# 32 unused columns behind the channel vectors of a two-layer hybrid encoder kernel: all tiles behind x lie 128 bytes further on

## The chip, the core and the metric

The kernel runs on one core of a Trainium2 chip. TensorE (PE in the profile) does the matrix products and loads their stationary operand with separate instructions (PEld). VectorE (DVE), ScalarE (ACT) and GpSimd (POOL) do the rest; SyncE (SP) issues most DMAs. On-chip memory (SBUF) has 128 partitions, and a tile takes the same stretch of addresses in each of them. The metric is the time of one execution on the device, in microseconds, lower is better.

## The reference

Two layers over 256 tokens of width 1024, then a last RMSNorm; all in float32:

```python
def hybrid_layer(x, ...):
    h = rms_norm(x, g_mix)
    proj = h @ w_in                                   # 1024 x 8704
    b_a, c_a, x_a, u_p, q, k, v, ga, gp, gt = jnp.split(proj, split_points(), axis=-1)
    y_a = short_conv_mixer(b_a, c_a, x_a, conv_w, w_a_out)
    y_p = multiscale_pool_mixer(u_p, w_pool, pool_scale)
    y_t = windowed_gqa(q, k, v, rel_bias, sink) @ w_attn_out
    merged = sigmoid(ga) * y_a + sigmoid(gp) * y_p + sigmoid(gt) * y_t
    x = x + merged @ w_o
    h2 = rms_norm(x, g_ffn)
    gate, up = jnp.split(h2 @ w_gu, [D_FF], axis=-1)
    return x + (silu(gate) * up) @ w_down
```

The convolution has three taps, the pool mixer averages over windows of 2 to 16 tokens, and the attention has 16 heads of 64 over 4 key heads.

## The kernel before, in words

**Layout.** The activations stand transposed: 128 channels on the partitions, 256 tokens along the row. The kernel cuts each weight matrix into blocks of 128 x 128; the host packs all blocks in the order of their use (`plan_layer`) into the array `wst`, 16 blocks (1 MB) to a chunk.

**Three products for one.** A float32 product is made of three matmuls in the rounded type float32r: a value is split into a rounded part (hi) and the rest (lo), and `mm3` (L163 to L167) adds W_hi·X_hi, W_hi·X_lo and W_lo·X_hi in PSUM. So each block of weights costs three matmuls of 256 columns, on L165, L166 and L167. Each matmul is preceded by a load of its weights. ScalarE and VectorE split the weights (`convert`, L131: raw to hi on ScalarE, raw minus hi to lo on VectorE) and the activations (`split`, L237).

**Order.** `take` walks over the plan; at each half chunk `advance` issues the DMAs of chunks to come (up to three raw buffers) and the conversion of half chunks to come (five hi and five lo buffers). The order of all other work is that of the program.

**Stages of a layer.** In the mixer: key and value projections, queries, gates, the convolution branch (c, y, z), the attention interleaved with it (`att_scores`, tile sc, L355 and L356, with weights in q and moving kk; `att_transpose`, tile pt, L384; `att_pv`, tile o, L399, with weights in vt and moving ph and pl), the pool branch (up, pp), and the merge (m, wo). Then the feed-forward part: gate and up from xg and h, down from fa (dn). The last layer's down projection has fa as its weights and moves hi and lo, 512 columns at a time (L625 to L627). While no normalised activations are there yet, the matmuls use xg, x times the norm's gain, and the norm's factor comes in later; afterwards they use h.

**Places in SBUF.** The pools are laid out in the order `const`, `wp`, `act`, `tmp`, each tile behind the one before. In bytes per partition: `wp` holds 3 raw tiles of 8192, 5 hi and 5 lo of 4096. `act` begins with the tile x (`xc`, L185): 2144 floats, that is 8576 bytes, the first 96 (`NG`) of them the channel vectors `ch` (gains, convolution taps and pool scales of both layers), the others the activations x, 8 x 256. Behind x come 8 tiles kk of 1024, 2 tiles up of 1088, 2 tiles vt of 2048, and then the pairs of 2048 bytes (a hi half and a lo half of 1024 each): xg, z and m (tag xz), q, ao and fa (tag q), ga and ya, h, pp. `tmp` follows with 8 tiles of 2048 (tag t2: s, ph, pl, sq, sg, fs and others), 10 of 1024 (tag t1), the bias tiles and small ones.

**Loads at the start.** `dma_chunk` for the first two chunks (L119 to L126) alternates pieces of x with pieces of the weights on SyncE's queue: first the channel vectors with the first 256 columns of x (L123), then four blocks of weights, and so on. In DRAM the array `xT` has one row per partition, laid out as the tile is.

Of the kernel before, what the change touches and what calls it, by code (L numbers as in the profile page):

```python
# [16 lines left out]
P = 128  # L17
D = 1024
T = 256
L = 2  # L20
KT = D // P
# [14 lines left out]
def plan_layer(last):  # L36

    out = []

    def inner(mat, ns, nk=KT):  # L40
        for n in ns:
            for k in range(nk):
                out.append((mat, k, n))

    def outer(mat, ns, nk=KT):
        for k in range(nk):
            for n in ns:
                out.append((mat, k, n))

    outer("in", (CK, CK + 1, CV, CV + 1))  # L50
    for q in range(2):
        inner("in", [CQ + 4 * q + j for j in range(4)])
    inner("in", [CGA + n for n in range(8)])
    for n in range(8):
        inner("in", (CC + n, CX + n, CB + n))
    inner("in", (CU, CU + 1))
    inner("a", range(8))
    for n in range(8):
        inner("in", (CGP + n, CGT + n))
        if n % 2 == 1 and n < 7:  # L60
            inner("in", (CU + n + 1, CU + n + 2))
        inner("t", (n,))
        out.extend(("pool", k, n) for k in range(2))
        if n >= 2:
            out.extend(("o", n - 2, m) for m in range(8))
    for j in range(4):
        out.extend(("o", k, m) for k in (6, 7) for m in (2 * j, 2 * j + 1))
    for q in range(NQ):
        ns = (2 * q, 2 * q + 1, FT + 2 * q, FT + 2 * q + 1)
        if q == 0:  # L70
            outer("gu", ns)
        else:
            inner("gu", ns)
        if q >= 1:
            for k in (2 * q - 2, 2 * q - 1):
                out.extend(("down", k, m) for m in range(8))
    ks = (2 * NQ - 2, 2 * NQ - 1)
    if last:
        for k in ks:
            out.extend(("down", k, m) for m in range(8))  # L80
    else:
        for j in range(4):
            out.extend(("down", k, m) for k in ks for m in (2 * j, 2 * j + 1))
    return out


NCH = len(plan_layer(False)) * L // CT
NG = L * 6 * KT


@with_exitstack
def trunk(ctx, tc, wst, xT, sinkb, rb, invc, gfin, ident_d, out):
# [24 lines left out]
    def dma_chunk(c):  # L117
        raw = wp.tile([P, CT * P], F32, name=f"raw{c}", tag="raw", bufs=3)
        if c < 2:  # L119
            for a, b, xa, xb in (((0, 4, 0, 1), (4, 8, 1, 2), (8, 16, 2, 4)), ((0, 8, 4, 6), (8, 16, 6, 8)))[c]:  # L120
                s = slice(0 if xa == 0 else NG + xa * T, NG + xb * T)
                if xa == 0:
                    nc.sync.dma_start(xc[:, s], xT[:, s])  # L123
                nc.sync.dma_start(raw[:, a * P:b * P], wst[c, :, a * P:b * P])
                if xa > 0:
                    nc.sync.dma_start(xc[:, s], xT[:, s])  # L126
        else:
            nc.sync.dma_start(raw, wst[c])
        raws[c] = raw
# [53 lines left out]
        PE.matmul(wps[:, :T], warm[:, :P], warm, start=True, stop=True)  # L183

    xc = act.tile([P, NG + KT * T], F32, name="x")  # L185
    ch = xc[:, :NG].rearrange("p (l g k) -> p l g k", l=L, g=6)
    x = xc[:, NG:].rearrange("p (k t) -> p k t", k=KT)
    dma_chunk(0)
    dma_chunk(1)
# [657 lines left out]
```

## Time and profile before

| | |
|---|---|
| runs shown | 986.62, 987.08 and 987.37 us, median 987.08 |
| the profiled execution | 987.34 us |
| its span, from first to last instruction | 985.2 us |
| granted TensorE clock, mean | 0.998 of full |
| HBM read | 175.80 MB, 180 GB/s over the span |
| hi and lo conversions of weights | 322 of each |
| DMA queue of SyncE: share of the 16 engines | 48.4% |

How to read the lines of the profile that follow. A group reads: line, engine, operation, what it writes <- what it reads (buffer numbers left out), shape written <- shape read, xcount | busy us, mean ns of one | idle time of the engine just before them, and what ended it. For a matmul the mean is from its start to its modelled end, so that it overlaps with the next; the pitch, from one start to the next, is shorter. In the windows view a row holds the stretch, its length, then busy time and count for PE, PEld, DVE, ACT and, where it has work, POOL, the granted clock, the DMA engines' share and GB/s; its last row holds the sums over the stretches. In the view of a single line or tile, three numbers with slashes are the shortest, the median and the longest duration in ns. In the timeline a row has start (us), duration (us), engine, line, operation, tiles and how many were merged. In the chain a row has start, duration and what it was.

### The profile page before, as it was taken

To read this page: it belongs to the slowest core of one execution; us is meant where nothing else is said; L and a number is where in the kernel's file an instruction comes from. 1 tells how busy PE (TensorE), PEld (TensorE's weight loads), DVE (VectorE), ACT (ScalarE), POOL (GpSimd) and SP (SyncE) were. 2 spreads that over 40 slices of the span, in tenths; PEclk is the share of its full clock that TensorE was granted. 3 is DMA by queue.
4 is the path that set the end of the run, shared out by engine and by line. 5 is a ranking of instruction groups with operands and counts; after the bars stand their busy time and mean duration, and the time that the engine had idled before them with its cause. 6 is when DMAs were issued, how large, how long until landed. Compare 5 with 4: busy or idle time off the path is not lost.

```text
span 985.2 us, 19117 instructions
## 1 busy us (share of the span) xinstructions
PE 975.4 (99%) x7881; PEld 963.1 (98%) x7881; DVE 712.6 (72%) x1277; ACT 553.5 (56%) x916; POOL 37.1 (4%) x60
## 2 busy tenths in 40 slices
PE   8999999999999999999999999999999999999997
PEld 8999999999999999999999999999999999999996
DVE  7899898577668955545589888975667697555555
ACT  6766666655456544444577566765544574444443
POOL 4000000000001000000020000000000020000000
PEclk9999999999999999999999999999999999999999
DMA  8656545544554555455543745444555455645531
GB/s 302 237 187 211 180 160 165 199 173 172 195 190 172 172 185 199 172 175 194 187 172 129 241 157 178 148 172 166 180 192 189 173 186 179 214 172 177 195 142 43
DMA packets 26967, 178.11 MB, mean 181 GB/s; under 512 B 3136, under 2 KB 3664, under 8 KB 6656
## 3 DMA queue, kind: packets, MB, share of 16 engines
q1 hardware_dynamic: 24768, 169.93, 48.4%
q0 software_dynamic: 2112, 6.97, 2.6%
q8 instruction: 61, 1.00, 0.4%
q14 instruction: 26, 0.21, 0.1%
HBM read 175.80 MB, written 1.08 MB: 180 GB/s over the span
## 4 chain that ended last, share of the span: by engine, by line
PE 98%; DMA 1%; DVE 0%; ACT 0%; SPq 0%; issue 0%
PE b L166 25%; PE b L165 25%; PE b L167 25%; PE dn L167 2%; PE dn L166 2%; PE dn L165 2%; PE dn L626 2%; PE dn L625 2%; PE dn L627 2%; PE wo L165 2%; PE wo L166 2%; PE o L399 2%; PE wo L167 2%; PE pt L384 1%; PE sc L356 1%; PE sc L355 1%
## 5 line engine op out<-in xcount | busy, mean ns | idle before, releaser
L139 DVE TENSOR_TENSOR lo<-raw,hi 128x1024 fp32r<-128x1024 f32 (+1 forms) x322 | 390.5, 1221 | 215.1 <-ACT hi L138 214.9
L138 ACT ACTIVATE hi<-raw 128x1024 fp32r<-128x1024 f32 (+1 forms) x322 | 337.1, 1053 | 337.5 <-PE b L166 213.1
L165 PE MATMUL b<-h,hi 128*128 128x256 f32 x1344 | 381.5, 284 | 0.0
L166 PE MATMUL b<-h,hi 128*128 128x256 f32 x1344 | 380.2, 283 | 0.0
L167 PE MATMUL b<-h,lo 128*128 128x256 f32 x1344 | 380.2, 283 | 0.0
L166 PEld LDWEIGHTS b<-h,hi 128*128 128x128 f32 x1344 | 257.9, 192 | 0.2
L165 PEld LDWEIGHTS b<-h,hi 128*128 128x128 f32 x1344 | 257.8, 192 | 0.2
L167 PEld LDWEIGHTS b<-h,lo 128*128 128x128 f32 x1344 | 257.8, 192 | 0.0
L166 PE MATMUL b<-xg,hi 128*128 128x256 f32 x448 | 127.0, 284 | 0.8 <-DVE xg L255 0.8
L165 PE MATMUL b<-xg,hi 128*128 128x256 f32 x448 | 127.2, 284 | 0.3 <-DVE xg L252 0.3
L167 PE MATMUL b<-xg,lo 128*128 128x256 f32 x448 | 126.8, 283 | 0.2 <-DVE lo L139 0.2
L166 PEld LDWEIGHTS b<-xg,hi 128*128 128x128 f32 x448 | 85.9, 192 | 1.4 <-DVE xg L255 1.3
L165 PEld LDWEIGHTS b<-xg,hi 128*128 128x128 f32 x448 | 85.8, 192 | 0.6 <-issue 0.5
L167 PEld LDWEIGHTS b<-xg,lo 128*128 128x128 f32 x448 | 85.9, 192 | 0.4 <-DVE lo L139 0.4
L165 PE MATMUL dn<-fa,hi 128*128 128x256 f32 x176 | 49.8, 283 | 0.0
L166 PE MATMUL dn<-fa,hi 128*128 128x256 f32 x176 | 49.8, 283 | 0.0
L167 PE MATMUL dn<-fa,lo 128*128 128x256 f32 x176 | 49.8, 283 | 0.0
L368 ACT ACTIVATE s<-s,sm 128x256 f32<-128x256 f32 x64 | 31.8, 499 | 13.0 <-DVE sm L363 13.0
L165 PE MATMUL b<-z,hi 128*128 128x256 f32 x128 | 36.5, 285 | 0.0
L165 PE MATMUL b<-ao,hi 128*128 128x256 f32 x128 | 36.2, 283 | 0.0
L166 PE MATMUL b<-ao,hi 128*128 128x256 f32 x128 | 36.2, 283 | 0.0
L167 PE MATMUL b<-ao,lo 128*128 128x256 f32 x128 | 36.2, 283 | 0.0
(176 smaller groups left out, 1500.5 us busy)
## 6 DMA issues: line engine op xcount, KB each, us to landing
raw<-wst SPq DMA_DIRECT2D x158, 1024.0 KB, 4.9
bias<-stab POOLq DMA_DIRECT2D x16, 384.0 KB, 4.2
raw<-wst SPq DMA_DIRECT2D x3, 512.0 KB, 8.0
out<-yg SPq DMA_DIRECT2D x4, 256.0 KB, 2.2
x<-xT SPq DMA_DIRECT2D x3, 256.0 KB, 8.0
raw<-wst SPq DMA_DIRECT2D x2, 256.0 KB, 4.6
gf<-gfin POOLq DMA_DIRECT2D x2, 256.0 KB, 2.9
x<-xT SPq DMA_DIRECT2D x1, 176.0 KB, 2.3
```

The lines of the kernel that those rows point to most:

```text
L138: S.activation(hi[:, s], raw[:, s], AF.Copy)
L139: V.tensor_tensor(lo[:, s], raw[:, s], hi[:, s].bitcast(F32), op=ALU.subtract)
L165: PE.matmul(dst, wh, xh, start=start, stop=False, skip_group_check=skip)
L166: PE.matmul(dst, wh, xl, start=False, stop=False, skip_group_check=skip)
L167: last_mm[0] = PE.matmul(dst, wl, xh, start=False, stop=stop, skip_group_check=skip)
L355: PE.matmul(ps[:, half(j)], qs[t][j][:, cs], kh, start=True, stop=False)
L356: PE.matmul(ps[:, half(j)], qs[t][j][:, cs], kl, start=False, stop=True)
L368: S.activation(ss[i // 2][:, i % 2], ss[i // 2][:, i % 2], AF.Exp, bias=sm[:, 4 + i:5 + i], accum_out=sm[:, 12 + i:13 + i])
L399: PE.matmul(ps[:, half(j)], vv, pts[kt][i][:, half(j)], start=(kt == i == 0), stop=(kt == i == 1))
L625: PE.matmul(d, ah[:, cs], wh, start=(k == 0), stop=False)
L626: PE.matmul(d, ah[:, cs], wl, start=False, stop=False)
L627: PE.matmul(d, al[:, cs], wh, start=False, stop=(k == FT - 1))
```

## The change

`NG` grows from 96 to 128 floats: the tile x gets 32 columns between the channel vectors and the activations that nothing reads. The channel vectors keep their place, the activations x and each tile allocated behind it move by 128 bytes per partition; const, raw, hi and lo stay. The host puts zeros into the same columns of `xT`, whose rows grow from 8576 to 8704 bytes. The first load of x takes the new columns along (384 floats per partition in place of 352). No instruction is added, removed or reordered.

```diff
-NG = L * 6 * KT
+
+NG = L * 6 * KT + 32
...
     xc = act.tile([P, NG + KT * T], F32, name="x")
-    ch = xc[:, :NG].rearrange("p (l g k) -> p l g k", l=L, g=6)
+    ch = xc[:, :L * 6 * KT].rearrange("p (l g k) -> p l g k", l=L, g=6)
     x = xc[:, NG:].rearrange("p (k t) -> p k t", k=KT)
...
-    xT = np.ascontiguousarray(np.concatenate([chp.reshape(P, NG), xT.reshape(P, KT * T)], axis=1))
+    xT = np.ascontiguousarray(np.concatenate([chp.reshape(P, L * 6 * KT), np.zeros((P, NG - L * 6 * KT), chp.dtype), xT.reshape(P, KT * T)], axis=1))
```

## The prediction

> **What bounds the kernel now.** I read the page first: span, busy times, granted clock, and the chain that ended last.
>
> ```profile
> span 985.2 us, 19117 instructions
> ...
> PE 975.4 (99%) x7881; PEld 963.1 (98%) x7881; DVE 712.6 (72%) x1277; ACT 553.5 (56%) x916; POOL 37.1 (4%) x60
> ...
> PEclk9999999999999999999999999999999999999999
> ...
> PE 98%; DMA 1%; DVE 0%; ACT 0%; SPq 0%; issue 0%
> ```
>
> TensorE is busy 99% of the time at the full granted clock, and the chain that sets the end runs over it for 98%. So only what TensorE itself needs per matmul can matter much; VectorE (72%) and ScalarE (56%) have room. How many matmuls of the main kind there are stands in the groups by line and shape:
>
> ```profile
> L165 PE MATMUL b<-h,hi 128*128 128x256 f32 x1344 | 381.5, 284 | 0.0
> ...
> L165 PE MATMUL b<-xg,hi 128*128 128x256 f32 x448 | 127.2, 284 | 0.3 <-DVE xg L252 0.3
> ...
> L165 PE MATMUL dn<-fa,hi 128*128 128x256 f32 x176 | 49.8, 283 | 0.0
> L165 PE MATMUL b<-z,hi 128*128 128x256 f32 x128 | 36.5, 285 | 0.0
> L165 PE MATMUL b<-ao,hi 128*128 128x256 f32 x128 | 36.2, 283 | 0.0
> ...
> L165 PE MATMUL wo<-m,hi 128*128 128x256 f32 x128 | 35.4, 284 | 0.0
> ...
> L165 PE MATMUL b<-pp,hi 128*128 128x256 f32 x32 | 9.1, 283 | 0.0
> ```
>
> These are 2384 on L165, and as many each on L166 and L167: 7152 matmuls of 256 columns. All have their weights in hi or lo and their moving operand in a tile behind x. One nanosecond more or less per matmul is 7.15 us, 0.72% of the time. This is the sensitivity on which everything below hangs.
>
> **The change, part by part.** It adds and removes no instruction, wait or queue entry. It makes the first x load larger, and it changes addresses. Take as a tile's *place* its distance behind the first weight tile, modulo 512 bytes, worked out from the tile sizes in the order of the pools. A weight block is 512 bytes wide, so every block of hi and lo is at place 0. Before, x begins at 0 and is 8 x 1024 + 384 bytes long, so the eight kk tiles are at 384; the two up tiles are 1088 bytes each, so vt and everything after (xg, z, m, q, ao, fa, h, pp, s, ph, pl) are at 384 + 2 x 64 = 512, that is 0 again. After, kk is at 0 and all those at 128. So today the weights and the moving operand of all 7152 matmuls begin at the same place, and after the change the moving operand begins 128 bytes off.
>
> Does TensorE see that? The trace holds a comparison of its own. The attention's P·V matmuls (L399, tile o) have weights in vt and move ph or pl: same place. The score matmuls (L355 and L356, tile sc) have weights in q and move kk: 384 against 0, that is 128 bytes off in the other direction. Both come in runs of 8, have 256 columns, use each weight block twice in a row, and are preceded by ordinary matmuls. The weight loads, by line and shape:
>
> ```profile
> L166 PEld LDWEIGHTS b<-h,hi 128*128 128x128 f32 x1344 | 257.9, 192 | 0.2
> ...
> L399 PEld LDWEIGHTS o<-ph,vt 128*128 128x128 f32 x64 | 12.3, 192 | 0.0
> ...
> L355 PEld LDWEIGHTS sc<-kk,q 128*128 128x128 f32 x64 | 12.1, 189 | 0.0
> ```
>
> 192 ns at the same place, 189 ns off it. For the pitch I take the busy time of TensorE on the tile kk alone and on vt alone, in windows that hold whole runs (first the stretch, then busy time and count):
>
> ```profile
> sum 210.00, PE 15.62 PEld 14.29 DVE 0.00 ACT 0.00; mean PE 7.81 PEld 7.15 DVE 0.00 ACT 0.00
> ```
>
> ```profile
> sum 260.00, PE 17.97 PEld 16.51 DVE 0.00 ACT 0.00; mean PE 8.98 PEld 8.26 DVE 0.00 ACT 0.00
> ```
>
> A run's busy time is seven pitches and the last matmul's own duration, whose median stands in the view of each line:
>
> ```profile
> L355 PE MATMUL sc<-kk,q x64: 279/282/285, 58.8 to 649.8; 128*128 128x256 f32 x64
> ```
>
> ```profile
> L399 PE MATMUL o<-ph,vt x64: 283/283/283, 78.9 to 669.9; 128*128 128x256 f32 x64
> ```
>
> The kk windows hold 14 runs: (15.62/14 - 0.282)/7 = 119.1 ns. The vt windows hold 16: (17.97/16 - 0.283)/7 = 120.0 ns. Moreover, o never varies (283/283/283), and sc does (279 to 285). I read this so: at the same place the loads of weights and the stream of the moving operand, which run at the same time, settle into one fixed rhythm of 120 ns that is a little slower than the free one; off it they don't. The same free rhythm shows for a moment after an interruption, in the timeline of TensorE (start, duration):
>
> ```profile
> 26.28 0.63 PE L303 MATMUL ps<-ident,rr 128*128 128x256 f32 x4
> 26.75 0.28 PE L165 MATMUL b<-xg,hi 128*128 128x256 f32 x1
> ...
> 27.70 0.28 PE L167 MATMUL b<-xg,lo 128*128 128x256 f32 x1
> ```
>
> From 26.28 to 27.70 there are 12 matmuls: 118.3 ns each. Afterwards they are back at 0.12.
>
> *Main matmuls.* Nearest row: sc, the one steady pattern with the operands 128 bytes apart. 7152 x (120.0 - 119.1) = 6.4 us less. Bounds: nothing, if the rhythm stays; 7152 x (120.0 - 118.3) = 12.2 us less, if the free rhythm lasts; and above, if each matmul took as long as sc's slowest (285 against 283), 7152 x 2 = 14.3 us more. I take 6.4.
>
> The Trainium skill speaks against this term: "TensorE: Matmul & The Clock Gate", section "Step-by-step: what each phase is for", says that TensorE reads its two operands from SBUF over independent ports and that loading the next weights takes nothing from the running matmul. By that this term is 0 and the time stays at 987.1. The trace does not quite agree: 119.1 against 120.0 ns between sc and o.
>
> *Other matmuls.* o: vt, ph and pl move together, no change. sc: q to 128, kk to 0, still 128 apart, no change. The last layer's down projection has its weights in fa, which moves, and its moving operand in hi, which doesn't:
>
> ```profile
> L625 PE MATMUL dn<-hi,fa 128*128 128x512 f32 x88 | 34.4, 390 | 0.0
> ...
> L625 PEld LDWEIGHTS dn<-hi,fa 128*128 128x128 f32 x88 | 16.6, 188 | 3.2
> ```
>
> Its weight loads are already at the short 188 ns, so I count 0; with 2 ns either way for its 264 it is 0.5 us.
>
> *VectorE, ScalarE, GpSimd.* Their operands move too. The hi and lo split of kk (place 384) and of h (place 0) tells whether they care:
>
> ```profile
> L239 DVE TENSOR_TENSOR h<-hf,h 128x256 fp32r<-128x256 f32 x32 | 12.3, 422 | 0.0
> ...
> L238 ACT ACTIVATE h<-hf 128x256 fp32r<-128x256 f32 x32 | 12.2, 413 | 5.3 <-DVE hf L314 5.1
> ...
> L239 DVE TENSOR_TENSOR kk<-kf,kk 64x256 fp32r<-64x256 f32 x8 | 3.4, 419 | 2.2 <-ACT kk L238 1.9
> L427 ACT ACTIVATE kk<-kf 64x256 fp32r<-64x256 f32 x8 | 3.3, 417 | 0.2
> ```
>
> 419 against 422 and 417 against 413 ns: no effect that shows. What could come late next is the weights' conversion, which shares these engines; at 72% and 56% busy it follows a matmul stream that is under 2% quicker. Without that cover the gain would stop there.
>
> *The loads at the start.* The first x load grows from 352 to 384 floats per partition, 176 to 192 KB, ahead of the weight loads in SyncE's queue; the chain and the issues:
>
> ```profile
> 2.59 6.40 DMA raw<-wst
> 9.02 0.64 ACT hi L138
> ```
>
> ```profile
> x<-xT SPq DMA_DIRECT2D x1, 176.0 KB, 2.3
> ```
>
> ```profile
> 0.00:30.00 30.00, 27.44 (x205) 26.43 (x206) 22.26 (x46) 19.22 (x29) 11.49 (x33) 1.00 0.91 322
> ```
>
> The chain waits for a raw load until 9.0 us, and the DMA engines move 322 GB/s meanwhile: 16.4 KB more is 0.05 us. Upper bound: in proportion to that load's 2.3 us, 0.2 us. Below, x's rows begin elsewhere in DRAM and SBUF; no row prices it, and I allow 0.2 us of gain. I take 0.05.
>
> *Sum.* The profiled execution took 987.34 us, 985.2 of it the span. 987.34 - 6.4 + 0.05 = 981.0. The median of the runs is 0.26 lower, hence 980.8, 0.6% faster.
>
> **The rivals.**
> *Longer free rhythm.* If the main stream runs free as it does after an interruption, 12.2 us: 975. For it: sc's runs are only 8 long and start out of the fixed rhythm. Against: that stretch falls back to 0.12 by itself.
> *Nothing changes.* The rhythm of 120 ns holds at any place, and sc differs for another reason, say that half of kk's partitions hold copies or zeros, or that runs of 8 are too short to settle. Or the change isn't what it says, since tiles are laid out otherwise than I worked out. Then 987.1. For it: almost all of the weight loads are at 192 ns, and after each interruption they return there. Against: o, from the same start, never leaves it, and sc leaves it each time.
> *Slower.* The main matmuls lock at another rhythm: the loads of weights collide with the moving stream for longer at +128 bytes, as sc has -128 and modulo 512 these differ. Place: L165 to L167. Price: up to 2 ns, sc's slowest duration, 14.3 us, so 1001; at half of that 994. It decides from a pitch over 120.3 ns, where 7152 x 0.3 is 0.2%. For it: sc reaches 285 ns. Against: its mean is lower.
>
> **How the numbers follow.** Forecast, 119.1 ns: 0.34. Free rhythm: 0.23. Nothing: 0.26. Slower: 0.17. The range goes from 973 (the free rhythm less 2 us for the starts and the last layer's matmuls) to 988.5 (nothing, and the bounds of the small terms), which leaves out the slower case and little else. About 0.2%, 2 us, is what a measurement of this kernel can tell from no change. Faster 0.57, same 0.26, slower 0.17.
>
> **What would show it.** If I am right, the weight loads of L165 to L167 fall from 192 to 187 to 190 ns, their matmuls' durations begin to vary, sc keeps 189 and 119.1, and the gain spreads evenly over the span, while the start (first 30 us) and the end stay. If the loads stay at 192 the time is unchanged. If they grow, the slower case has come. The forecast is wrong if the gain comes from the start, or if VectorE's or ScalarE's groups change their mean.

## The result, and the profile after

| | before | after |
|---|---|---|
| median on the device | 986.93 us (986.62 to 987.37, 4 runs) | 979.87 us (979.42 to 980.07, 4 runs) |
| span of the profiled execution | 985.2 us | 977.7 us |

The ratio is 0.9927, with a 95% interval of 0.991 to 0.9945: 0.7% faster. The forecast was 980.8 us.

The page of the changed kernel, in the lines that answer to those shown of before:

```profile
span 977.7 us, 19117 instructions
...
PE 968.2 (99%) x7881; PEld 954.9 (98%) x7881; DVE 712.1 (73%) x1277; ACT 552.7 (57%) x916; POOL 38.0 (4%) x60
...
PEclk9999999999999999999999999999999999999999
...
PE 98%; DMA 1%; DVE 0%; ACT 0%; SPq 0%; issue 0%
```

The same instructions, the same clock, the same bound. TensorE's busy time fell from 975.4 to 968.2 us, which is the gain; VectorE and ScalarE kept theirs. (The kernel has one line more ahead of them, so L165 to L167 are now L166 to L168, and L625 to L627 are L626 to L628.) Groups by line and shape:

```profile
L166 PEld LDWEIGHTS b<-h,hi 128*128 128x128 f32 x1344 | 253.2, 188 | 0.2
...
L400 PEld LDWEIGHTS o<-ph,vt 128*128 128x128 f32 x64 | 12.2, 191 | 0.0
...
L356 PEld LDWEIGHTS sc<-kk,q 128*128 128x128 f32 x64 | 12.0, 188 | 0.0
```

The weight loads of the main matmuls take 188 ns in place of 192. Those of o, whose two operands moved together, are nearly unchanged at 191. The view of one line tells the same of the matmuls (shortest, median, longest, ns). First the main ones on one line before and after, then o after; before, o was at 283/283/283:

```profile
L166 PE MATMUL b<-h,hi x1344: 280/283/283, 68.6 to 966.7; 128*128 128x256 f32 x192
```

```profile
L167 PE MATMUL b<-h,hi x1344: 274/281/287, 68.1 to 958.8; 128*128 128x256 f32 x192
```

```profile
L400 PE MATMUL o<-ph,vt x64: 281/283/283, 78.3 to 663.4; 128*128 128x256 f32 x64
```

The main matmuls vary now, as sc did; o still has its median of 283. How much it brings is in the busy time on single tiles. First h, the sum over the span, before and after:

```profile
sum 990.00, PE 494.98 PEld 488.22 DVE 12.29 ACT 12.24; mean PE 247.49 PEld 244.11 DVE 6.15 ACT 6.12
```

```profile
sum 990.00, PE 490.09 PEld 483.25 DVE 12.22 ACT 12.21; mean PE 245.04 PEld 241.62 DVE 6.11 ACT 6.11
```

4.89 us less for 4032 matmuls: 1.2 ns each. Then fa, in the first layer, where it is the moving operand (528 matmuls of 256 columns), and in the second, where it is the weights (264 matmuls of 512 columns), before and after:

```profile
0.00:500.00 500.00, 64.99 (x528) 64.08 (x528) 8.30 (x22) 7.80 (x22) 1.00 0.54 189
500.00:990.00 490.00, 61.75 (x264) 48.92 (x264) 8.30 (x22) 7.80 (x22) 0.99 0.48 171
```

```profile
0.00:500.00 500.00, 64.28 (x528) 63.35 (x528) 8.29 (x22) 7.79 (x22) 1.00 0.54 191
500.00:990.00 490.00, 62.91 (x264) 49.03 (x264) 8.29 (x22) 7.80 (x22) 1.00 0.47 169
```

The first layer gains 0.71 us, 1.3 ns per matmul; the second *loses* 1.16 us, 4.4 ns per matmul. The same view gives 1.78 us of gain for xg and 1.55 for z, ao, m and pp. Together: 4.89 + 1.78 + 1.55 + 0.71 = 8.9 us gained on the 7152 matmuls, 1.2 lost in the last down projection, 0.1 gained on sc and o. That makes 7.8; the span shrank by 7.5. Of the difference, the first long raw load accounts for 0.1 (6.50 us, before 6.40), as the chain shows; 0.2 is not assigned:

```profile
2.59 6.50 DMA raw<-wst
...
9.12 0.64 ACT hi L139
```

### The profile page after: what moved, and what is told of

The parts are those of the page before. It is cut to its first block, busy times and chain, and to the rows that moved or that the text cites. A ratio compares the mean times of both kernels' runs of the same rounds, so it can differ in the third digit from the quotient of the medians.

```text
span 977.7 us, 19117 instructions
## 1 busy us (share of the span) xinstructions
PE 968.2 (99%) x7881; PEld 954.9 (98%) x7881; DVE 712.1 (73%) x1277; ACT 552.7 (57%) x916; POOL 38.0 (4%) x60
## 4 chain that ended last, share of the span: by engine, by line
PE 98%; DMA 1%; DVE 0%; ACT 0%; SPq 0%; issue 0%
PE b L168 25%; PE b L167 25%; PE b L166 25%; PE dn L168 2%; PE dn L167 2%; PE dn L166 2%; PE dn L628 2%; PE dn L627 2%; PE dn L626 2%; PE wo L166 2%; PE wo L167 2%; PE o L400 2%; PE wo L168 2%; PE pt L385 1%; PE sc L356 1%; PE sc L357 1%
## 5 line engine op out<-in xcount | busy, mean ns | idle before, releaser
L166 PE MATMUL b<-h,hi 128*128 128x256 f32 x1344 | 379.8, 283 | 0.0
L168 PE MATMUL b<-h,lo 128*128 128x256 f32 x1344 | 378.4, 282 | 0.0
L167 PE MATMUL b<-h,hi 128*128 128x256 f32 x1344 | 378.3, 281 | 0.0
L166 PEld LDWEIGHTS b<-h,hi 128*128 128x128 f32 x1344 | 253.2, 188 | 0.2
L167 PEld LDWEIGHTS b<-h,hi 128*128 128x128 f32 x1344 | 253.1, 188 | 0.2
L168 PEld LDWEIGHTS b<-h,lo 128*128 128x128 f32 x1344 | 253.1, 188 | 0.0
L167 PE MATMUL b<-xg,hi 128*128 128x256 f32 x448 | 126.3, 282 | 0.9 <-DVE xg L256 0.9
L166 PE MATMUL b<-xg,hi 128*128 128x256 f32 x448 | 126.6, 283 | 0.2 <-DVE xg L253 0.2
L168 PE MATMUL b<-xg,lo 128*128 128x256 f32 x448 | 126.2, 282 | 0.0
L167 PEld LDWEIGHTS b<-xg,hi 128*128 128x128 f32 x448 | 84.4, 188 | 1.3 <-DVE xg L256 1.3
L166 PEld LDWEIGHTS b<-xg,hi 128*128 128x128 f32 x448 | 84.3, 188 | 0.4 <-ACT hi L139 0.3
L168 PEld LDWEIGHTS b<-xg,lo 128*128 128x128 f32 x448 | 84.3, 188 | 0.1
L168 PE MATMUL dn<-fa,lo 128*128 128x256 f32 x176 | 49.5, 281 | 0.0
L167 PE MATMUL dn<-fa,hi 128*128 128x256 f32 x176 | 49.5, 281 | 0.0
L166 PE MATMUL dn<-fa,hi 128*128 128x256 f32 x176 | 49.5, 281 | 0.0
L166 PE MATMUL b<-z,hi 128*128 128x256 f32 x128 | 36.4, 284 | 0.0
L168 PE MATMUL b<-z,lo 128*128 128x256 f32 x128 | 36.1, 282 | 0.0
L168 PE MATMUL b<-ao,lo 128*128 128x256 f32 x128 | 36.0, 282 | 0.0
L166 PE MATMUL b<-ao,hi 128*128 128x256 f32 x128 | 36.0, 281 | 0.0
```

The source lines that it names most:

```text
L166: PE.matmul(dst, wh, xh, start=start, stop=False, skip_group_check=skip)
L167: PE.matmul(dst, wh, xl, start=False, stop=False, skip_group_check=skip)
L168: last_mm[0] = PE.matmul(dst, wl, xh, start=False, stop=stop, skip_group_check=skip)
```

## The experiments

**Theory:** what counts is the distance, that is how far the moving operand's address in a partition lies behind that of the weights, modulo 512 bytes as the prediction has it. **Rivals:** the loads at the start and the longer rows of xT; the moving tiles' own address; any move at all. All are edits of the kernel before or after; all compute the whole reference. Four kernels tell them apart.

**e_tile_only** moves the tiles and leaves the loads as they were.

```diff
-    xc = act.tile([P, NG + KT * T], F32, name="x")
+    xc = act.tile([P, NG + KT * T + 32], F32, name="x")
-    x = xc[:, NG:].rearrange("p (k t) -> p k t", k=KT)
+    x = xc[:, NG:NG + KT * T].rearrange("p (k t) -> p k t", k=KT)
```

> The 32 columns stand at the end of the tile x, behind the activations, and not in DRAM: kk and everything behind it move by 128 bytes, x itself, the rows of xT and the loads at the start are as in the kernel before. Theory (distance of the moving operand from the weights): weight loads of b<-h at 188 ns, pitch 118.7, about 980 us, ratio 0.993. Rival (the gain comes from the loads at the start or from the rows of xT): 987 us, weight loads at 192 ns.

Measured: 979.87 us, ratio 0.9926 (0.9912 to 0.9941), the whole effect. In its groups:

```profile
L167 PEld LDWEIGHTS b<-h,lo 128*128 128x128 f32 x1344 | 253.0, 188 | 0.0
```

**e_dram_only** is the counterpart: the changed kernel, with `+ 96` columns at the end of the tile x (where e_tile_only has `+ 32`). So the loads at the start are those of the change, while the tiles behind x lie 512 bytes further on than before, which modulo 512 is distance 0 again.

> The change with 96 more columns at the end of the tile x: rows of xT, first load and place of x as in the changed kernel, but kk and all behind it lie 512 bytes further on than in the kernel before, so that h, xg, fa and the others are back at the weights' place modulo 512. Theory: 120.0 ns, weight loads at 192 ns, 987 us. Rival (loads at the start, rows of xT): 980 us. Rival (tiles have only to move, by any amount): 980 us.

Measured: 987.6 us, ratio 1.0003 (0.9993 to 1.0012):

```profile
L168 PEld LDWEIGHTS b<-h,lo 128*128 128x128 f32 x1344 | 257.8, 192 | 0.0
```

The loads at the start and xT's rows bring nothing, and a move of the moving tiles by 512 bytes doesn't either.

**e_shift_all** moves both operands.

```diff
-    epst = const.tile([P, 1], F32, name="epst")
+    epst = const.tile([P, 33], F32, name="epst")[:, 0:1]
```

> The kernel before with a constant tile ahead of the weights' tiles longer by 128 bytes: raw, hi, lo, x and everything behind move by 128 bytes together. Theory (only the distance between the two operands counts): 120.0 ns, weight loads at 192 ns, 987 us. Rival (the moving tiles' own address counts, the same as in the changed kernel): 980 us, weight loads at 188 ns.

Measured: 987.42 us, ratio 1.0001 (0.9992 to 1.0011). The weights lie where no kernel so far had them, and by the tile sizes the moving tiles behind x lie exactly where the changed kernel has them, but the gain is gone and the loads are back at 192 ns. So the moving tiles' own address isn't what counts:

```profile
L167 PEld LDWEIGHTS b<-h,lo 128*128 128x128 f32 x1344 | 257.8, 192 | 0.0
```

**e_cols_64** asks for the period; `NG` has 64 more columns.

```diff
-NG = L * 6 * KT + 32
+NG = L * 6 * KT + 64
```

> The change with 64 columns, 256 bytes, in place of 32. If the pattern repeats after 256 bytes: 120.0 ns, weight loads at 192 ns, 987 us. If it repeats after 512 bytes or more: another free rhythm with loads near 188 ns, 978 to 982 us.

Measured: 987.9 us, ratio 1.0007 (0.9997 to 1.0017), weight loads at 192 ns, the longest of the matmuls on h 283 ns: 256 bytes off is the same as 0. My prediction had counted places modulo 512; from here on distances are given modulo 256, which is shown at this one distance and taken for the others.

That raised the next question: is 128 bytes the best distance, or just one that isn't 0? I went on in steps of 32 bytes. Besides 0, a period of 256 bytes has seven such distances, and six of them were untried. Each is `NG = L * 6 * KT + n` with another n.

> 8 columns, 32 bytes, in place of 32 columns. Theory (the fixed rhythm needs the same distance of both operands modulo 256 bytes, exactly): free rhythm, weight loads near 188 ns, pitch about 118.7, 980 us. Rival (a fixed rhythm holds over a band of distances around 0): 192 ns, 120.0, 987 us.

> 16 columns, 64 bytes. Theory: free rhythm, about 980 us. Rival (only half the period breaks the rhythm): 987 us. A distance at which the two streams meet more often than at 0 would be slower, up to 122 ns and 1001 us.

> 24 columns, 96 bytes. Theory: free rhythm, about 980 us. Rivals: 987 us (fixed at 120.0), or slower than that if this distance meets more often.

> 48 columns, 192 bytes, which modulo 256 is 64 bytes off in the other direction. Theory: the pitch of 64 bytes if only the size of the distance counts, another one if its sign counts too; between 978 and 987 us.

> 40 columns, 160 bytes, which modulo 256 is 96 bytes off in the other direction. If only the size of the distance counts: the time of 24 columns, 989 us. If the sign counts: between 961 and 987 us, the pitch to be read from the trace.

> 56 columns, 224 bytes, 32 bytes off in the other direction. If only the size counts: the time of 8 columns, 966 us. If the sign counts: between 961 and 990 us.

> 48 columns once more, beside its neighbours: 961 to 966 us, ratio 0.974 to 0.978.

| columns | distance, bytes mod 256 | time, us | ratio (95%) | busy on h, us | last down projection, us |
|---|---|---|---|---|---|
| 0 (before) | 0 | 986.93 | 1 | 494.98 | 61.75 |
| 8 | 32 | 966.16 | 0.9785 (0.9771 to 0.98) | 481.95 | 63.20 |
| 16 | 64 | 970.17 | 0.9822 (0.9807 to 0.9837) | 482.87 | 63.23 |
| 24 | 96 | 989.02 | 1.0015 (1.0006 to 1.0025) | 494.99 | 63.37 |
| 32 (the change) | 128 | 979.87 | 0.9927 (0.991 to 0.9945) | 490.09 | 62.91 |
| 40 | 160 | 973.22 | 0.9858 (0.9844 to 0.9871) | 485.45 | 63.23 |
| 48 | 192 | 963.87 | 0.9738 (0.9719 to 0.9758) | 482.68 | 62.36 |
| 48 again | 192 | 965.79 | 0.9766 (0.9742 to 0.9791) | 481.89 | 62.30 |
| 56 | 224 | 977.77 | 0.9902 (0.9889 to 0.9915) | 488.46 | 63.21 |
| 64 | 0 | 987.9 | 1.0007 (0.9997 to 1.0017) | 494.97 | 61.76 |

Each ratio is taken against executions of the kernel before that were run beside that kernel (their medians are 986.93 to 987.58 us). In the last column the weights are in fa, the tile that moves, so there the distance has the opposite sign. (One of the four executions with 48 columns took 2435.82 us, the others 961.14, 961.95 and 965.8. Why is not known. The time in the table is the median of all four; the ratio leaves that one out.)

Four of my expectations fell. "Free rhythm, about 980" was wrong for 8 and 16 columns, which gain two to three times as much as the change, and for 24, which gains nothing; and 48 columns, expected at 978 to 987 us, took less than 966 in three of four executions. The sign of the distance counts as well: 32 and 224 differ, and so do 96 and 160. So there isn't one fixed rhythm and one free one; the pitch differs from distance to distance. Windows over the same 70 us, at the end of the first mixer and the start of the feed-forward part, show it; a larger count in the same time is a shorter pitch. In order: before (distance 0), after (128 bytes), 8 columns (32 bytes), 24 columns (96 bytes).

```profile
200.00:270.00 70.00, 70.00 (x585) 70.00 (x585) 46.82 (x79) 34.38 (x48) 0.00 (x0) 1.00 0.52 184
```

```profile
200.00:270.00 70.00, 70.00 (x592) 70.00 (x591) 47.40 (x81) 35.22 (x49) 0.00 (x0) 1.00 0.54 195
```

```profile
200.00:270.00 70.00, 70.00 (x602) 70.00 (x601) 49.91 (x88) 35.36 (x50) 0.00 (x0) 1.00 0.53 185
```

```profile
200.00:270.00 70.00, 70.00 (x585) 70.00 (x585) 46.85 (x78) 34.01 (x48) 0.00 (x0) 1.00 0.53 187
```

About 2.4 matmuls of each count only reach into the window from its edge (a matmul's record lasts 0.283 us). So 70/582.6 = 120.1 ns before, 70/589.6 = 118.7 after, 70/599.6 = 116.7 with 8 columns and 120.1 again with 24. The last case is instructive, because its matmuls vary and its loads are mostly short all the same:

```profile
L168 PEld LDWEIGHTS b<-h,lo x1344: 187/187/193, 68.3 to 967.6; 128*128 128x128 f32 x192
L168 PE MATMUL b<-h,lo x1344: 277/281/286, 68.4 to 967.7; 128*128 128x256 f32 x192
```

The start times in its trace, to the nanosecond, show that in the long stretches the pitches repeat as 116, 123, 119, 120, 117, 125 ns. Their mean is 120.0; other orders, in shorter stretches, have means of 119.7 to 120.0. A load of 188 ns, or a varying matmul, is therefore no sign of a gain; only the pitch is.

With 192 bytes two pitches follow one another within one execution (48 columns):

```profile
25.00:55.00 30.00, 30.00 (x266) 30.00 (x266) 27.78 (x54) 23.56 (x44) 0.00 (x0) 1.00 0.58 219
200.00:230.00 30.00, 30.00 (x257) 30.00 (x257) 20.30 (x33) 15.13 (x22) 0.00 (x0) 1.00 0.53 191
```

30/263.6 = 113.8 ns early on, and 30/254.6 = 117.8 later. By the start times, a stretch of main matmuls that nothing interrupts keeps one of two rhythms to its end, about 113.3 to 113.9 ns or 117.8, and only after an interruption (scores, sums, transposes) the other can follow. 64 bytes has the same two, here in 24 us each:

```profile
509.00:533.00 24.00, 24.00 (x214) 24.00 (x213) 23.50 (x46) 17.61 (x32) 0.00 (x0) 1.00 0.41 136
195.00:219.00 24.00, 24.00 (x206) 24.00 (x205) 17.81 (x33) 13.26 (x19) 0.00 (x0) 1.00 0.54 182
```

24/(214 - 2.5) = 113.5 ns and 24/(206 - 2.4) = 117.9. So 64 and 192 bytes don't differ in their rhythms but in how long each holds: of the main matmuls in stretches of 40 or more, 17% ran in the faster one at 64 bytes and 26% at 192. At 160 bytes there are two as well (117.3 and 118.7 ns), and the changed kernel, otherwise at 118.7, ran two stretches of 94 at 120.0. Executions that enter the faster rhythm more often could explain the wide spread with 48 columns, 960.04 to 967.8 us in six executions; only one execution of each run has a trace, so that isn't shown.

**e_weights_moved** moves the weights against the moving tiles: raw, hi and lo by 64 bytes, the moving tiles by 256.

```diff
-    epst = const.tile([P, 1], F32, name="epst")
+    epst = const.tile([P, 17], F32, name="epst")[:, 0:1]
-    xc = act.tile([P, NG + KT * T], F32, name="x")
+    xc = act.tile([P, NG + KT * T + 48], F32, name="x")
-    x = xc[:, NG:].rearrange("p (k t) -> p k t", k=KT)
+    x = xc[:, NG:NG + KT * T].rearrange("p (k t) -> p k t", k=KT)
```

> The constant tile ahead of the weights longer by 64 bytes and the tile x by 192 at its end: raw, hi and lo move by 64 bytes, kk and all behind it by 256, so that modulo 256 the moving tiles lie where they lay in the kernel before and the weights don't. The moving operand is then 192 bytes off the weights, as with 48 columns. Theory (distance): 961 to 966 us, pitch about 116.7. Rival (the moving tiles' own address): 987 us, 120.0.

Measured: 962.43 us (958.6 to 966.17), ratio 0.9734 (0.9704 to 0.9763), with busy time on h at 481.58 us. The moving tiles lie modulo 256 where they lay before the change, and the gain is that of 48 columns. With e_shift_all this settles that the distance counts and the address alone does not, as far as these distances go. It and 48 columns are faster than both kernels, by 2.3 to 2.7% against before; between these two the runs show no difference.

## Why the prediction was right, point by point

- **The bound, and the sensitivity.** Right. Nothing but TensorE's pitch moved, over the whole span.
- **The main term** was mis-sized: I took 0.9 ns per matmul from sc, 6.4 us in all. Measured are 1.2 to 1.3 ns and 8.9 us. That lies between the term's two rows, sc and the stretch after an interruption (12.2 us). The row was the right one, but I took its mean over too short a run. By the start times in the trace, the seven pitches of an sc run before are about 119, 122, 120, 119, 115, 118 and 121.5 ns, and the main matmuls after the change repeat about 119, 115, 118, 122, 120. So sc already ran in the pattern of five that the main matmuls then took up, and its seven pitches are one whole pattern and two more, 119 and 121.5. The five of one pattern have a mean of 118.7, which would have given 7152 x 1.3 = 9.3 us. (sc lies 128 bytes off in the other direction, which modulo 256 is the same distance.) In the other row, four of the twelve matmuls are L303's, on other operands; the eight ordinary ones took 118.4 ns each. After the change sc has a pitch of (15.53/14 - 0.281)/7 = 118.3 ns, from this sum of the windows on kk; I had expected that it keeps 119.1.

```profile
sum 207.00, PE 15.53 PEld 14.28 DVE 0.00 ACT 0.00; mean PE 7.77 PEld 7.14 DVE 0.00 ACT 0.00
```

- **The last layer's down projection** was counted at 0, with 0.5 us either way; it lost 1.2 us. The reason I gave, that its loads were at 188 ns already, was a wrong sign to go by: they still are, and it is slower. The main term was 2.5 us too small and this one 1.2 us the other way, so the two errors partly cancel; that the total came out within 1 us is in part luck. (The terms add up to 980.7 us; I wrote 980.8.)
- **The loads at the start** at 0.05 us: 0.1 measured on the first raw load, and e_dram_only finds no difference in the whole time.
- **VectorE and ScalarE** not affected: right, within about 1% (h's split 417 and 412 ns after, 422 and 413 before).
- **The reading behind it**, a fixed rhythm at distance 0 that any distance breaks, was right for 0 and 256 and for 128 as a gain, and too simple: what I called free is a steady pattern of five pitches, and at 96 bytes another steady pattern has the same mean pitch of 120.0 ns, where I would have forecast a gain too.
- **The rivals.** "Nothing changes" was answered by the o and sc rows in the way forecast: o stayed, the main matmuls went the way of sc. The longer free rhythm was as near as my forecast: the 118.7 ns of the windows lies between its 118.3 and my 119.1, and the 8.9 us between its 12.2 and my 6.4. The slower case did not come: its sign was a pitch over 120.3 ns, and no distance has one. The kernel with 24 columns is 0.15% slower than before, but its main matmuls keep 120.0 ns; it loses in the last down projection (63.37 us against 61.75).
- **The Trainium skill**, "TensorE: Matmul & The Clock Gate", section "Step-by-step: what each phase is for", says that TensorE reads its two operands from SBUF over independent ports and that loading the next weights takes no read bandwidth from the running matmul. By that I had a main term of 0 as the alternative; the runs do not agree with that 0: the pitch depends on where the two operands lie to each other, 116.7 ns at 32 bytes and 120.1 at 0. Whether the two reads meet at a port they do not show.

**Still open:** what makes the period of 256 bytes and the order of the pitches; why some distances have two rhythms and which interruption leads to which; distances finer than 32 bytes, and a separate best distance for the last down projection, neither of which was tried.

## What to carry to other kernels

Where TensorE is busy 99% of the time with a weight load for each matmul, compare the pitch of groups whose operands lie differently in SBUF; a difference of 1 ns in 120, with the same shapes, is a sign that the layout may count. Then try several distances between the weights and the moving tiles by a pad, here in steps of 32 bytes: it costs no instruction, it was worth from -0.15% to 2.7%, and neither the size nor the sign of the distance foretold which. A layout that changes for another reason can win or lose that much as well, so time a change of tile sizes against the same change with the distance kept.

## What the runs showed of the hardware that I had not expected

- The pitch of a 256-column float32r matmul with a weight load each ran from 113.8 to 120.1 ns in the windows shown, at a granted clock of 1.00, by the distance of the operands to each other; moving both together by 128 bytes changed nothing (ratio 1.0001).
- It settles into repeating patterns, of one step (120 at distance 0), of five (118.7 on average at 128 bytes) or of six (120.0 at 96 bytes). At 64 and 192 bytes it takes one of two rhythms, 113.3 to 113.9 or 117.8 ns, and keeps it until an interruption.
- The 512-column matmuls of the last down projection were fastest at distance 0 (61.75 us for 264) and lost up to 1.6 us elsewhere, while the 256-column ones were slowest at 0 and at 96 bytes.
- A weight load's duration (188 or 192 ns) does not tell the pitch: 188 ns went with 116.7, with 118.7 and with 120.1.
